# Memory rows transposed raw, their norm's gains in the weight tiles, and split memory kept in DRAM for a second layer

## The chip, the cores and the metric

The kernel runs on one core of one Trainium2 chip. The metric is the device time of one execution in microseconds (us), lower is better. A core has TensorE (PE, matmuls; PEld loads its weights), VectorE (DVE), ScalarE (ACT), GpSimd (POOL) and SyncE (SP, which here only issues DMA transfers). Each works through a row of instructions fixed when the program is built, and semaphores hold an instruction until what it reads is there.

## The reference, cut to what matters

Two encoder layers over x (512 tokens, D = 1024). In each, a token mixer and a cross attention of 4 heads to 256 memory tokens share one input projection and one output projection. The part that the change touches is the memory's way into K and V:

```python
def rmsnorm(x, g):
    y = x * lax.rsqrt(jnp.mean(x * x, axis=-1, keepdims=True) + EPS)
    return y * g
...
for i in range(DEPTH):
    h = rmsnorm(x, norm_g[i])
    mem_h = rmsnorm(mem, mem_norm_g[i])
    ...
    o_mem = memory_attention(q_mem, mem_h, w_mem_kv[i], mem_qn_g[i], mem_kn_g[i])
    y = jnp.concatenate([o_mix, o_mem], axis=-1) * jax.nn.silu(gate)
    x = x + jnp.einsum('bse,ed->bsd', y, w_out[i])
...
def memory_attention(q_mem, mem_h, w_kv, qn_g, kn_g):
    kv = jnp.einsum('bnd,de->bne', mem_h, w_kv).reshape(Bn, N, 2, MEM_HEADS, HEAD_DIM)
    k = rmsnorm(kv[:, :, 0], kn_g)
    v = kv[:, :, 1]
```

mem_norm_g has one row of 1024 gains for each layer; memory itself is the same in both layers. The norm of a memory row is a factor for each token (rm) and a gain for each of the 1024 features.

## The kernel before

All products are f32. Each operand is split in a high and a low part (fp32r), and a product is three matmuls: high times high and low times high of the activations (lines 176 and 177, mm_early), later high times the weights' low part (line 180, mm_late). The weights, 258 tiles of 128x1024 (`wl`), stream from DRAM over SP's queue (line 261). ACT casts a tile to its high part `wh` (line 323, Weights.hi), DVE subtracts to get the low part `wo` (line 333, Weights.lo); four such pairs are kept (RING). Some tiles are sums or differences of weight blocks, made by transfers from POOL that add in place (lines 261, 297 and 307).

A driver written in Python sets the order of every engine's row: matmul groups tick slots, and generators spawned with a delay (`drv.spawn`) put their next instructions in at a slot. A weight load is issued when the number of live tiles falls below a table's (KEEP).

The program begins with the memory. SP loads a row of gains and memory in pieces (lines 1056 to 1060), weights between them, then x's gains (line 654) and x's four tiles (line 1068). PE spreads the gains' row over the partitions by matmuls with ones (`spread`, line 1118). DVE multiplies memory by it (`times`, line 1128), PE transposes the product (`turn4`, line 536, into `xT`), and the result is split into `act` (`split`, lines 164 to 167; by `place_m`). ACT sums the squares of each memory row (`square`, line 1132) and POOL makes the tokens' factors of them (`factor`, lines 1137 to 1140: `rm` holds each factor plain, times QS and times 0.5). The factor of a token is applied behind the product, to K's sums of squares (line 629) and to V (line 707, `ev_v`). `mem_kv` runs eight groups of twelve 128x512 matmuls on `act`, each followed by its eviction. The transposes and splits of memory's four blocks are put between these groups by `ahead`; those of x (`prep`: squares in line 523, POOL's `rstd`, the product with `rstd` and gains in line 530, transposes) follow.

In the second layer `mem_norm(1)`, spawned during the first layer's output projection, loads memory and its gains again, normalizes it in full on DVE (line 530 into `m`), transposes it (16 transposes, in PE's row among the output projection's matmuls) and splits it; `mem_kv(1, ...)` then uses no factor.

Of the kernel before, what the change touches and what calls it, by code (L numbers as in the profile page):

```python
# [10 lines left out]
F32 = mybir.dt.float32  # L11
# [19 lines left out]
PD = 2  # L31
EO = 2, 2, 1, 2, 2, 1
# [99 lines left out]
def trunk_kernel(ctx: ExitStack, tc: tile.TileContext, x, mem, wall, norm_g, mem_norm_g, gcol,  # L132
# [63 lines left out]
    class Weights:  # L196
# [66 lines left out]
        def dma(self, most=9):  # L263
            while self.allocs and self.live < KEEP_C.get(self.allocs[0][0][0], KEEP[self.allocs[0][2]]) and most:
# [7 lines left out]
                self.load(nc.sync, self.tile[key], d)  # L272
# [40 lines left out]

        def hi(self, force=False):
# [8 lines left out]
            A.copy(wh, self.tile[self.items[i]])  # L323
            self.hi_at.append(self.g)
            self.op.append((wh, wo))
            return True

        def lo(self):
            i = self.n_lo
            self.n_lo += 1  # L330
            wh, wo = self.op[i]
            key = self.items[i]
            V.tensor_tensor(wo, self.tile[key], wh.bitcast(F32), ALU.subtract)  # L333
            self.lo_at[key] = self.g
            self.use(key)
# [153 lines left out]
    gc = pool.tile([128, 10], F32, name="gc")  # L489
    gk = pool.tile([128, 3], F32, name="gk")  # L490
# [5 lines left out]
    ones = tabs[0:1, 0:128]  # L496
    V.memset(half, -0.5)
    V.memset(ones, 1.0)
    A.activation(small.tile([128, 1], F32, tag="sm1", name="warm"), half[:, 0:1], AF.Exp)

    class Act:


        def __init__(self, n):
            per = 1024 // n
            self.tiles = [[m4(F32R, "act").rearrange("p (k t) -> p k t", k=per) for _ in range(8 // per)] for _ in range(2)]
# [152 lines left out]
    def mem_norm(layer):  # L659
        row_load("m", mem_norm_g[layer:layer + 1, :])  # L660
        t = [m4(name="m") for _ in range(2)]
        for b in range(2):
            nc.sync.dma_start(t[b], mem[b * 128:(b + 1) * 128])
        t = [halves(v) for v in t]
        yield MEM_D
        norm_2(t[0], rm[:, 0:1], rows["m"])
        yield 1
        norm_2(t[1], rm[:, 1:2], rows["m"])
        M = Act(NM)
        for b in range(2):  # L670
            for j in range(2):
                norm_3(t[b], M, b * 128, j)
            yield 1
        Ms[layer] = M

# [8 lines left out]
    def mem_kv(layer, M, mid=None):  # L684
# [4 lines left out]
        def ev_k(b, p):  # L689
            r = head_sq(p) if layer else head_sq(p, by=rm[:, 2 + b:3 + b])  # L690

            def rest():
                if not layer:
                    G.tensor_scalar(r, r, rm[:, b:b + 1], None, ALU.mult)
# [9 lines left out]
        def ev_v(b, p):  # L704

            t = s2(name="vr") if layer else raw[:, b * 512:b * 512 + 512]
            A.activation(t, p, AF.Copy, scale=0.5 if layer else rm[:, 4 + b:5 + b])
# [346 lines left out]
    nc.scalar.dma_start(ident, ident_d)  # L1054
    row0 = m4(name="row0")[0:1, :]
    nc.sync.dma_start(row0, mem_norm_g[0:1, :])
    nc.sync.dma_start(mt[0][:, 0:512], mem[0:128, 0:512])
    W.dma(2)
    nc.sync.dma_start(mt[1], mem[128:256])
    nc.sync.dma_start(mt[0][:, 512:1024], mem[0:128, 512:1024])  # L1060
    W.dma(2)
    row_load("x", norm_g[0:1, :])
    W.dma(2)
# [3 lines left out]
    for c in range(4):  # L1067
        nc.sync.dma_start(xt[c], xv[c])
        if c % 2 and c < 3:
            W.dma(2)  # L1070
# [41 lines left out]
    row = [at("row") for _ in range(2)]  # L1112

    def spread(j, *cols):

        for c in cols:
            cs = slice(256 * c, 256 * c + 256)
            T.matmul(row[j][:, cs], ones, row0[:, 512 * j + 256 * c:512 * j + 256 * c + 256], start=True, stop=True, skip_group_check=True)

    spread(0, 0, 1)  # L1120
    mb, M = [halves(t) for t in mt], Act(NM)
    ss = [sm(2, "ss") for _ in range(2)]
    mg = {}

    def times(b, j):

        t = mg[b, j] = s2(name="mg")
        V.tensor_tensor(t, mb[b][j], row[j], ALU.mult)
# [13 lines left out]
    def place_m(b, j, act=True, p=None):  # L1142

        cs = slice(b * 128, (b + 1) * 128)
        split(M.block(0, j, cs), M.block(1, j, cs), p or turn4(mg[b, j], None, None), act)
# [12 lines left out]
    for b, j in ((1, 0), (0, 1), (1, 1)):  # L1158
        square(b, j)
    for b in range(2):  # L1160
        times(b, 1)
        factor(b)

    def ahead(u, b):
# [5 lines left out]
        if (u, b) == (0, 1):  # L1170
            place_m(0, 1)
            place_m(1, 1)

    drv.spawn(prep(), PD)
# [293 lines left out]
    drv.spawn(mem_norm(1), MEM_B)  # L1468
# [318 lines left out]
```

## Time and profile before

| what | value |
|---|---|
| time before, median of 3 runs | 941.91 us (941.63 to 941.92) |
| profiled execution: time / span | 942.24 us / 940.5 us |
| PE busy | 932.8 us, 99% |
| DVE / ACT / POOL busy | 798.6 / 691.3 / 346.0 us |
| PE busy in the first 23.5 us | 21.01 us |
| DMA | 207.15 MB, mean 220 GB/s; 354 GB/s in the first 23.5 us |

In the rows below, a timeline row begins with the start in us and the time the row spans, then engine, line, operation, what is written and read, shapes and count; in brackets stands the idle time before it and what ended it. A row of several instructions (x4) is one block. A matmul's duration runs past the start of the next one, so the distance of two starts is what a matmul costs. A row of the windows has, for each engine, the busy time and the count, then the granted clock, the DMA share (1.0 and more is full) and GB/s.

### The profile page before, as it was taken

What the parts mean: (1) busy time and instruction counts of PE and PEld (TensorE: products, weight loads), DVE (VectorE), ACT (ScalarE), POOL (GpSimd) and SP (SyncE); (2) the same over time, 40 slices, a digit from 0 to 9 for tenths busy, and PEclk for the clock granted to TensorE, in tenths of its full rate; (3) what the DMA queues carried; (4) which work ended last, traced back from release to release, by engine and by line L of the source; (5) the groups of instructions that cost most, each with busy time, mean ns of one, the idle gap of its engine ahead of it and who ended that gap; (6) DMA issues with size and microseconds to landing.
All of it is one profiled execution on the core that took longest, in us unless ns stands there. A gap on an engine that the chain in (4) does not pass through costs nothing.

```text
span 940.5 us, 16300 instructions
## 1 busy us (share of the span) xinstructions
PE 932.8 (99%) x5500; PEld 819.9 (87%) x5500; DVE 798.6 (85%) x1442; ACT 691.3 (74%) x1720; POOL 346.0 (37%) x494
## 2 busy tenths in 40 slices
PE   8999999999999999999999999999999999999998
PEld 6889888888888888888889998888988999999886
DVE  6898676879888888889788899977998998689977
ACT  7775788677768686867675667637878887789774
POOL 3411425455554545463836111114262440111123
PEclk9999999999999999999999999999999999999999
DMA  9999937869787878696867889979985686785777
GB/s 355 386 259 336 299 91 190 278 139 256 158 250 147 260 154 268 158 268 136 249 165 206 246 200 243 305 229 326 270 203 122 166 239 168 199 221 126 190 173 179
DMA packets 89429, 207.15 MB, mean 220 GB/s; under 512 B 25217, under 2 KB 34689, under 8 KB 89346
## 3 DMA queue, kind: packets, MB, share of 16 engines
q1 hardware_dynamic: 68818, 140.64, 43.4%
q0 software_dynamic: 19520, 63.97, 36.9%
q10 hardware_dynamic: 1008, 1.51, 0.4%
q8 instruction: 43, 0.70, 0.3%
q14 instruction: 40, 0.33, 0.1%
HBM read 158.31 MB, written 11.08 MB: 180 GB/s over the span
## 4 chain that ended last, share of the span: by engine, by line
PE 91%; DVE 4%; DMA 3%; ACT 1%; issue 0%; SPq 0%; DVEq 0%; ACTq 0%
PE pj L176 24%; PE pj L177 24%; PE pj L180 23%; PE qT L641 2%; DMA og<-od 2%; PE ptb L1616 1%; PE sa L1302 1%; PE oo L1410 1%; PE pt L1389 1%; DMA wl<-in_wall_dram 1%; PE xT L536 1%; PE sa L1298 1%; DVE wo L333 1%; PE ob L180 1%; PE ob L177 1%; PE ob L176 1%
## 5 line engine op out<-in xcount | busy, mean ns | idle before, releaser
L333 DVE TENSOR_TENSOR wo<-wl,wh 128x1024 fp32r<-128x1024 f32 x258 | 316.4, 1232 | 7.0 <-ACT wh L323 6.8
L323 ACT CAST wh<-wl 128x1024 fp32r<-128x1024 f32 x258 | 271.7, 1060 | 29.7 <-PE pj L177 15.6
L176 PE MATMUL pj<-wh,hS 128*128 128x512 f32 (+1 forms) x416 | 154.3, 380 | 0.0
L177 PE MATMUL pj<-wh,hS 128*128 128x512 f32 (+1 forms) x416 | 148.9, 367 | 0.0
L176 PE MATMUL pj<-wh,h 128*128 128x512 f32 (+1 forms) x312 | 115.2, 378 | 0.0
L177 PE MATMUL pj<-wh,h 128*128 128x512 f32 (+1 forms) x312 | 111.7, 367 | 0.0
L484 POOL TENSOR_TENSOR rstd<-mse,half 128x4 f32<-128x4 f32 (+2 forms) x98 | 103.0, 1051 | 8.2
L180 PE MATMUL pj<-wo,hS 128*128 128x512 f32 (+1 forms) x416 | 99.5, 366 | 0.0
L177 PEld LDWEIGHTS pj<-wh,hS 128*128 128x128 f32 x416 | 78.7, 189 | 11.3
L176 PEld LDWEIGHTS pj<-wh,hS 128*128 128x128 f32 x416 | 78.6, 189 | 11.1 <-DVE sn L420 0.2
L483 POOL TENSOR_SCALAR mse<-hss 128x4 f32<-128x4 f32 (+1 forms) x88 | 46.1, 524 | 103.2 <-ACT junk L629 95.5
L180 PEld LDWEIGHTS pj<-wo,hS 128*128 128x128 f32 x416 | 72.4, 189 | 13.1
L629 ACT ACTIVATE junk<-sn 128x128 f32<-128x128 f32 x264 | 79.3, 311 | 2.2 <-DVE sn L411 2.1
L1246 POOL TENSOR_TENSOR ta<-sn,tabs 128x128 f32<-128x128 f32 (+1 forms) x64 | 35.9, 567 | 120.1 <-DVE sn L634 92.8
L398 ACT COPY sn<-pj 128x512 f32<-128x512 f32 x122 | 67.2, 590 | 16.6 <-PE pj L180 15.8
L180 PE MATMUL pj<-wo,h 128*128 128x512 f32 (+1 forms) x312 | 74.5, 365 | 0.0
L307 POOL DMA_DIRECT2D wl<-wl x34 | 30.2, 898 | 114.8 <-DVE wo L333 74.6
L261 POOL DMA_DIRECT2D wl<-in_wall_dram x40 | 38.1, 968 | 81.6 <-DMA wl<-in_wall_dram 35.3
L420 DVE TENSOR_TENSOR sn<-pj,sn 128x512 f32<-128x512 f32 x89 | 60.8, 684 | 7.1 <-PE pj L180 6.6
L177 PEld LDWEIGHTS pj<-wh,h 128*128 128x128 f32 x312 | 59.0, 189 | 8.4
L176 PEld LDWEIGHTS pj<-wh,h 128*128 128x128 f32 x312 | 59.0, 189 | 8.2
L180 PEld LDWEIGHTS pj<-wo,h 128*128 128x128 f32 x312 | 54.3, 189 | 9.7
(283 smaller groups left out, 2366.7 us busy)
## 6 DMA issues: line engine op xcount, KB each, us to landing
wl<-in_wall_dram SPq DMA_DIRECT2D x224, 512.0 KB, 7.5
wl<-wl POOLq DMA_DIRECT2D x68, 512.0 KB, 5.5
wl<-in_wall_dram POOLq DMA_DIRECT2D x44, 512.0 KB, 8.3
od<-o SPq DMA_DIRECT2D x11, 256.0 KB, 5.1
og<-od SPq DMA_DIRECT2D x10, 256.0 KB, 9.8
x<-in_x_dram SPq DMA_DIRECT2D x4, 512.0 KB, 9.0
v0d<-sn SPq DMA_DIRECT2D x8, 256.0 KB, 10.5
acc<-in_x_dram POOLq DMA_DIRECT2D x8, 256.0 KB, 7.1
```

The source lines that it names most:

```text
L176: T.matmul(o, a, b, start=start, stop=False, skip_group_check=True)
L177: T.matmul(o, c, d, start=False, stop=False, skip_group_check=True)
L180: T.matmul(o, a, b, start=False, stop=stop, skip_group_check=True)
L261: queue.dma_start(t, wall[d], **how)
L323: A.copy(wh, self.tile[self.items[i]])
L333: V.tensor_tensor(wo, self.tile[key], wh.bitcast(F32), ALU.subtract)
L398: A.copy(t, b)
L420: V.tensor_tensor(t, b, t, ALU.subtract if q == "12" else ALU.add)
L483: G.tensor_scalar(e, ss, EPS, None, ALU.add)
L484: G.tensor_tensor(r, e, half[:, 0:n], ALU.pow)
L629: A.activation(jk, p[:, j * 128:(j + 1) * 128], AF.Square, scale=by, accum_out=ss[:, j:j + 1])
L1246: G.tensor_tensor(ta[:, 0:n], xn[:, 0:n, 0:32], ropeA[:, 0, b, s0:s0 + n], ALU.mult)
```

## The change

- Memory is transposed raw. The row of gains, its eight spreading matmuls and the four products on DVE go away. The gains of both layers are loaded as 16 rows of 128 (`gm`), transposed once by PE (`gt`) and copied into `gmc`: one column for each 128 features.
- The gains go into the memory's weight tiles: a tile of 128x1024 holds two blocks of features, so ACT makes `wh` in two halves with a scale column each, and DVE makes `wo` in two halves as weights times gain minus `wh`. There are 16 such tiles, 8 in each layer.
- The token's factor is now applied in both layers behind the product; POOL multiplies K's factor by `rm` in the second layer too (two small operations).
- The split memory of the first layer (four `act` tiles, 512 KB each) is written to DRAM (`md`) by `keep_m`, and `mem_again` reads it back for the second layer. Its two memory loads, row of gains, norm, 16 transposes and splits go away.
- The first transfers are smaller: half a weight tile, a quarter of memory, the second half, and then weight tiles and quarters of memory in turn; x's gains come behind six weight tiles.
- The identity is made by POOL (affine_select) on cleared columns instead of being loaded. PE runs six matmuls on the cleared columns first (WARM).
- The first block of memory is cast and subtracted in two halves; the squares of memory go behind the third and fourth block's transposes. At most 10 weight tiles are live up to the third slot (START_KEEP).

The diff, cut to its core:

```diff
+WARM, START_KEEP, KEEP_M = 6, 10, 5
 ...
-            A.copy(wh, self.tile[self.items[i]])
+            key = self.items[i]
+            if key[1] == "P" and PLAN[key[0]] != "O1":
+                for c, g in self.gains(key):
+                    A.activation(wh[:, c], self.tile[key][:, c], AF.Copy, scale=g)
+            else:
+                A.copy(wh, self.tile[key])
 ...
+                for c, g in self.gains(key):
+                    V.scalar_tensor_tensor(wo[:, c], self.tile[key][:, c], g, wh[:, c].bitcast(F32), ALU.mult, ALU.subtract)
 ...
-    def mem_norm(layer):
 ...
+    def mem_again():
+        M = Ms[1] = Act(NM)
+        for n, t in enumerate(M.flat):
+            nc.sync.dma_start(t.bitcast(F32), md[n])
+        yield 1
 ...
-    nc.scalar.dma_start(ident, ident_d)
+    nc.scalar.dma_start(gm, mem_norm_g.rearrange("l (k p) -> (l k) p", p=128))
+    G.affine_select(ident, zero, [[-1, 128]], ALU.not_equal, 1.0, base=0, channel_multiplier=1)
 ...
+    for _ in range(WARM):
+        T.matmul(idle[:, 0:128], zero, zero, start=True, stop=True, skip_group_check=True)
+    T.transpose(gt, gm, ident[0:16, 0:16])
+    V.tensor_copy(gmc, gt)
 ...
-    square(0, 0)
-    times(0, 0)
-    spread(1, 0)
-    p = turn4(mg[0, 0], None, None)
-    spread(1, 1)
     W.hi(True)
-    place_m(0, 0, False, p)
     W.hi(True)
+    place_m(0, 0, (slice(0, 2), slice(2, 4)), False)
     W.lo()
-    times(1, 0)
     W.lo()
-    for b, j in ((1, 0), (0, 1), (1, 1)):
-        square(b, j)
-    for b in range(2):
-        times(b, 1)
-        factor(b)
 ...
         if (u, b) == (0, 1):
             place_m(0, 1)
+            square(0, 0)
+            square(0, 1)
+            factor(0)
+        if (u, b) == (1, 0):
             place_m(1, 1)
+            square(1, 0)
+            square(1, 1)
+            factor(1)
+    def keep_m():
+        for n, t in enumerate(M.flat):
+            nc.sync.dma_start(md[n], t.bitcast(F32))
+            yield 2
+    drv.spawn(keep_m(), KEEP_M)
 ...
-    drv.spawn(mem_norm(1), MEM_B)
+    drv.spawn(mem_again(), MEM_B)
```

Three places of the rows, before and after. First ACT from its first transfer to the squares of the first keys (`junk`); `sq` are squares of memory (`m`) and of `x`, `act` are the casts of memory's blocks. Before:

```order
L1054 DMA ident<-in_ident_dram 128x128
L1132 ACTIVATE sq,ss<-m 128x512
L323 CAST wh<-wl 128x1024 x2
L1132 ACTIVATE sq,ss<-m 128x512 x3
L164 CAST act<-xT 128x4x128
L323 CAST wh<-wl 128x1024 x2
L164 CAST act<-xT 128x4x128 x2
L323 CAST wh<-wl 128x1024 x2
L523 ACTIVATE sq,ss<-x 128x512 x4
L629 ACTIVATE junk,hss<-pj,rm 128x128 x4
```

After:

```order
L1067 DMA gm<-in_mem_norm_g_dram 16x128
L337 ACTIVATE wh<-wl,gmc 128x512 x4
L165 CAST act<-xT 128x4x128
L337 ACTIVATE wh<-wl,gmc 128x512 x4
L165 CAST act<-xT 128x4x128
L1141 ACTIVATE sq,ss<-m 128x512 x2
L337 ACTIVATE wh<-wl,gmc 128x512 x4
L546 ACTIVATE sq,ss<-x 128x512 x2
L165 CAST act<-xT 128x4x128
L1141 ACTIVATE sq,ss<-m 128x512 x2
L546 ACTIVATE sq,ss<-x 128x512 x2
L652 ACTIVATE junk,hss<-pj,rm 128x128 x4
```

The squares of memory and the casts of the weights have changed places with the casts of memory's blocks: the last of these now stands behind the squares of x's first tile.

Then DVE in the same stretch, where the last row is the product of x's first tile. Before:

```order
L1128 TENSOR_TENSOR mg<-m,row 128x512
L166 CAST act<-xT 128x4x128
L167 TENSOR_TENSOR act<-xT,act 128x4x128
L333 TENSOR_TENSOR wo<-wl,wh 128x1024
L1128 TENSOR_TENSOR mg<-m,row 128x512
L333 TENSOR_TENSOR wo<-wl,wh 128x1024
L1128 TENSOR_TENSOR mg<-m,row 128x512 x2
L167 TENSOR_TENSOR act<-xT,act 128x4x128
L333 TENSOR_TENSOR wo<-wl,wh 128x1024 x2
L167 TENSOR_TENSOR act<-xT,act 128x4x128 x2
L333 TENSOR_TENSOR wo<-wl,wh 128x1024 x2
L530 SCALAR_TENSOR_TENSOR x<-x,rstd,row 128x512 x2
```

After:

```order
L1135 COPY gmc<-gt 128x16
L167 CAST act<-xT 128x2x128
L168 TENSOR_TENSOR act<-xT,act 128x2x128
L167 CAST act<-xT 128x2x128
L168 TENSOR_TENSOR act<-xT,act 128x2x128
L351 SCALAR_TENSOR_TENSOR wo<-wl,gmc,wh 128x512 x4
L168 TENSOR_TENSOR act<-xT,act 128x4x128
L351 SCALAR_TENSOR_TENSOR wo<-wl,gmc,wh 128x512 x4
L168 TENSOR_TENSOR act<-xT,act 128x4x128 x2
L351 SCALAR_TENSOR_TENSOR wo<-wl,gmc,wh 128x512 x4
L553 SCALAR_TENSOR_TENSOR x<-x,rstd,row 128x512 x2
```

The products of memory and gains are gone, and each pair of weight tiles is four halves. As before, the last two subtractions of memory's blocks stand together, ahead of the third pair of tiles, and these ahead of x's product; the second subtraction reads what ACT's last cast of memory writes.

Last SP, from the loads of x's four tiles to the first store of v0 (`v0d`, which waits for data of the first values of x). Before:

```order
L1068 DMA x<-in_x_dram 128x1024 x2
L261 DMA wl<-in_wall_dram 128x1024 x2
L1068 DMA x<-in_x_dram 128x1024 x2
L261 DMA wl<-in_wall_dram 128x1024 x18
L1183 DMA v0d<-sn 128x512 x2
L261 DMA wl<-in_wall_dram 128x1024
```

After:

```order
L1087 DMA x<-in_x_dram 128x1024 x2
L262 DMA wl<-in_wall_dram 128x1024 x2
L1087 DMA x<-in_x_dram 128x1024 x2
L262 DMA wl<-in_wall_dram 128x1024 x14
L1186 DMA md<-act 128x1024 x2
L262 DMA wl<-in_wall_dram 128x1024 x2
L1186 DMA md<-act 128x1024
L262 DMA wl<-in_wall_dram 128x1024
L1186 DMA md<-act 128x1024
L262 DMA wl<-in_wall_dram 128x1024
L1199 DMA v0d<-sn 128x512 x2
L262 DMA wl<-in_wall_dram 128x1024
```

The four writes of `act` to `md` stand among the last weight loads ahead of that store. On PE, at the boundary of the layers, the two rows of eight transposes of `m` (line 536), each behind a group of twelve matmuls of the output projection, are gone; nothing else in that stretch of PE's row changes.

More of the change, by code (lines that the diff above doesn't have):

```diff
@@ L312, in sum, with gains @@
             return False
+        def gains(self, key):
+            n = 8 * (PLAN[key[0]] == "T2b") + 2 * key[2]
+            return [(slice(512 * h, 512 * h + 512), gmc[:, n + h:n + h + 1]) for h in range(2)]
         def hi(self, force=False):
@@ L489, in trunk_kernel @@
     gc = pool.tile([128, 10], F32, name="gc")
+    gmc = pool.tile([128, 16], F32, name="gmc")
     gk = pool.tile([128, 3], F32, name="gk")
@@ L505, in __init__ @@
             per = 1024 // n
-            self.tiles = [[m4(F32R, "act").rearrange("p (k t) -> p k t", k=per) for _ in range(8 // per)] for _ in range(2)]
+            self.flat = [m4(F32R, "act") for _ in range(16 // per)]
+            ts = [t.rearrange("p (k t) -> p k t", k=per) for t in self.flat]
+            self.tiles = [ts[:8 // per], ts[8 // per:]]
             self.part = [[t[:, k] for t in ts for k in range(per)] for ts in self.tiles]
@@ L1110, in setup @@
             yield 1
[L1112 to L1120, printed above, removed]
+    idle, gt = at("idle"), at("gt")[:, 0:16]
+    for _ in range(WARM):
+        T.matmul(idle[:, 0:128], zero, zero, start=True, stop=True, skip_group_check=True)
+    T.transpose(gt, gm, ident[0:16, 0:16])
+    V.tensor_copy(gmc, gt)
     mb, M = [halves(t) for t in mt], Act(NM)
     ss = [sm(2, "ss") for _ in range(2)]
[L1123 to L1128, printed above, removed]
     def square(b, j):
```

68 lines of the change are left out of this document (33 added, 35 removed).

## The prediction

> **What bounds the kernel.** I read the page's first two parts, then the waits of TensorE (PE) over the whole span, then the timeline of the engines where PE is not busy, which is the start.
>
> ```profile
> span 940.5 us, 16300 instructions
> ...
> PE 932.8 (99%) x5500; PEld 819.9 (87%) x5500; DVE 798.6 (85%) x1442; ACT 691.3 (74%) x1720; POOL 346.0 (37%) x494
> ```
>
> ```profile
> PE row L1118 <- DMA row<-in_mem_norm_g_dram: 2.3, 1, 2.3
> PE pmt L768 <- DVE pmT L774: 0.7, 1, 0.7
> ```
>
> PE is busy in 99% of 940.5 us. It waits 2.3 us for the first row and at no other place more than 0.7 us, so a change counts only where it takes matmuls out of PE's row, or moves PE's first 24 us. The row of each engine is fixed when the program is built; an engine that waits holds all that stands behind it.
>
> The start on PE:
>
> ```profile
> 2.26 2.89 PE L1118 MATMUL row<-row,tabs 1*128 1x256 f32 x6 [2.26 <-DMA row<-in_mem_norm_g_dram]
> 5.08 1.11 PE L536 MATMUL xT<-ident,mg 128*128 128x128 f32 x4
> ...
> 7.28 0.80 PE L176 MATMUL pj<-wh,act 128*128 128x512 f32 x1
> 7.87 0.63 PE L177 MATMUL pj<-wh,act 128*128 128x512 f32 x1
> ...
> 10.43 0.63 PE L177 MATMUL pj<-wh,act 128*128 128x512 f32 x1
> 10.86 1.05 PE L536 MATMUL xT<-ident,mg 128*128 128x128 f32 x4
> 11.56 1.42 PE L180 MATMUL pj<-wo,act 128*128 128x512 f32 x4
> 12.82 0.39 PE L176 MATMUL pj<-wh,act 128*128 128x512 f32 x1
> ...
> 15.03 1.03 PE L536 MATMUL xT<-ident,mg 128*128 128x128 f32 x8
> ...
> 16.83 0.39 PE L176 MATMUL pj<-wh,act 128*128 128x512 f32 x1
> ...
> 19.70 0.39 PE L176 MATMUL pj<-wh,act 128*128 128x512 f32 x1
> ...
> 21.52 1.07 PE L180 MATMUL pj<-wo,act 128*128 128x512 f32 x4
> 22.71 1.06 PE L536 MATMUL xT<-ident,x 128*128 128x128 f32 x8
> 23.53 0.48 PE L176 MATMUL pj<-wh,act 128*128 128x512 f32 x1
> ```
>
> The eight row matmuls (2.26 and, the last two, 6.13) and the transposes fill PE until the first real matmul at 7.28. The groups of twelve matmuls (hi times both parts of the memory, then four with the weights' low part) that make the memory's K and V start at 7.28, 12.82, 16.83, 19.70, then 23.53: call them G0 to G4. From 7.28 to 10.43 a matmul of 128x512 comes every 0.43 us ((10.43 - 7.87)/6), and in G3 every 0.23 ((21.52 - 19.70)/8); the four from 11.56 take 0.32 each. So PE's clock came up near 12 us, 4.7 us after G0's start. Between G3's end and G4 stand the transposes of x's first tile, at 22.71; they wait for VectorE. From 23.5 on there is hardly a gap, so what G4 gains or loses the end gains or loses.
>
> The same stretch on ScalarE (ACT) and VectorE (DVE):
>
> ```profile
> 3.81 0.63 ACT L1132 ACTIVATE sq<-m 128x512 f32<-128x512 f32 x1 [1.59 <-DMA m<-in_mem_dram]
> ...
> 6.17 1.04 ACT L323 CAST wh<-wl 128x1024 fp32r<-128x1024 f32 x1 [1.64 <-DMA wl<-in_wall_dram]
> 7.47 1.04 ACT L323 CAST wh<-wl 128x1024 fp32r<-128x1024 f32 x1 [0.25 <-DMA wl<-in_wall_dram]
> ...
> 11.95 0.59 ACT L164 CAST act<-xT 128x512 fp32r<-128x512 f32 x1 [1.19 <-PE xT L536]
> 12.43 2.00 ACT L323 CAST wh<-wl 128x1024 fp32r<-128x1024 f32 x2
> 15.72 1.07 ACT L164 CAST act<-xT 128x512 fp32r<-128x512 f32 x2 [1.29 <-issue]
> ...
> 18.58 0.64 ACT L523 ACTIVATE sq<-x 128x512 f32<-128x512 f32 x1
> ...
> 19.20 0.63 ACT L523 ACTIVATE sq<-x 128x512 f32<-128x512 f32 x1
> ```
>
> ```profile
> 6.24 0.69 DVE L166 CAST act<-xT 128x512 fp32r<-128x512 f32 x1 [1.21 <-PE xT L536]
> 6.96 0.69 DVE L167 TENSOR_TENSOR act<-xT,act 128x512 fp32r<-128x512 f32 x1
> 7.57 1.21 DVE L333 TENSOR_TENSOR wo<-wl,wh 128x1024 fp32r<-128x1024 f32 x1
> ...
> 21.18 1.43 DVE L530 SCALAR_TENSOR_TENSOR x<-x,rstd,row 128x512 f32<-128x512 f32 x2 [1.05 <-POOL rstd L484]
> ```
>
> ACT is free between 7.47 and 11.95 but for squares; DVE's last wait before G4 is for x's statistics (21.18).
>
> **The change, part by part.**
>
> *First transfers and row matmuls, a gain at G0.* The first matmul now needs half a weight tile, a quarter of the memory and no row. The first quarter of memory was there at 3.81 and the first weight tile, 512 KB further in the queue, at 6.17, so 256 KB cost 1.2 us here; with half a weight tile going first and 0.4 us earlier, memory lands at about 4.6 and the weight's second half at 5.8. Transposes at 4.6 need no product with the row (mg, 0.69 us). From 5.08 to 6.24 the transposes took 1.16; the high part is now made in two halves (0.35 each), and G0 starts at 4.6 + 1.16 + 0.4 = 6.2, say 6.3: 1.0 us earlier. G0 needs the tables of gains on the partitions (gmc), which take the place of the identity's transfer and come before 4 us; the identity itself is made by POOL.
>
> *G1.* G0 to G1 took 5.54 (12.82 - 7.28), most of it at the slow clock. If the clock counts from the first real matmul, G1 starts at 6.3 + 5.5 = 11.8, less about 0.2 us for the second row matmuls that no longer press: 11.6, a gain of 1.2. If the six idle matmuls at about 1 us bring the clock up earlier, G1 is at 10.8; if the clock comes up no earlier than it did, at 12.4.
>
> *ACT's row between G1 and G4, a loss.* Weight tiles of the memory are now scaled in halves. A half with a scale taken from a tile has no row at the start; the nearest of its size, squares, follow each other in 0.62 us (18.58, 19.20), so four halves are about 2.4 us where two whole casts took 2.0 (12.43). More than that, the row's order changes. After the cast of the third block of memory come two squares of memory, four halves for the next two weight tiles, two squares of x, and only then the cast of the fourth block, on which G3 depends; before, both casts stood together at 15.72. So, from G1 = 11.6: the third block's transposes stand behind G1's eight matmuls, 2.2 us later (12.82 to 15.03), its cast 0.7 us behind these (15.03 to 15.72), at 14.5; cast 0.6, squares 1.2, four halves 2.4, squares 1.2: the fourth block's cast starts at 19.9. Even if PE were faster, it stands behind x's first tile: 7.5 tiles of 512 KB follow the second weight tile, which lands near 7.4, at 1.30 us each (6.17 to 7.47): 17.2, and two squares end at 18.4. G3 starts about 0.7 us behind the cast: 20.6 (19.1 at the least), against 19.70.
>
> *DVE's row behind it.* The subtraction of that block (0.6, as from 6.96 to 7.57) is followed by four halves of wo. One half is a product with a scalar and a subtraction, as x's in row 21.18: two in 1.43, 0.69 apart; four take 2.8, where two whole ones took 2.4. Only then comes x's product. The cast at 19.9 frees it at 20.5; 20.5 + 0.6 + 2.8 = 23.9 is x's start instead of 21.18. Row 21.18 to row 23.53 is 2.35, so G4 starts at 26.2: 2.7 us later than before. The fastest case (the cast at 18.4, set by x's landing) gives 19.0 + 0.6 + 2.8 + 2.35 = 24.75, +1.2; the slowest (G1 at 12.4) 27.0, +3.5. I take +2.6, a little under the middle value, since an early clock weighs more than a late one.
>
> *Second layer's memory, a gain.* At the boundary stand 2 x 8 transposes of m, in PE's row without a gap:
>
> ```profile
> 615.28 1.07 PE L180 MATMUL pj<-wh,y 128*128 128x512 f32 x4
> 616.19 1.03 PE L536 MATMUL xT<-ident,m 128*128 128x128 f32 x8
> 616.98 0.48 PE L176 MATMUL pj<-wh,y 128*128 128x512 f32 x1
> 617.29 0.40 PE L177 MATMUL pj<-wo,y 128*128 128x512 f32 x1
> ```
>
> Four matmuls from 615.28 end their pitch at 616.19; the next matmul comes at 616.98 and the one behind it 0.31 later where the pitch is 0.23. So eight transposes are 0.79 + 0.08 = 0.87 us, sixteen 1.74. The products, casts and subtractions that leave DVE and ACT there gain nothing, PE not waiting for them; the weight tiles' halves there cost 0.2 us of ACT and of DVE per tile, hidden behind the casts and subtractions that leave. The second layer reads four tiles (2 MB) instead of 1.5 MB, far ahead of use.
>
> *Memory kept in DRAM, a small loss.* The first layer writes 2 MB more, from SP's queue, ahead of the last four weight loads before the first store of v0:
>
> ```profile
> 15.80 22.46 SPq L261 DMA_DIRECT2D wl<-in_wall_dram  x18
> 53.70 0.92 SPq L1183 DMA_DIRECT2D v0d<-sn  x2
> ```
>
> ```profile
> 23.50:47.00 23.50, 23.50 (x119) 19.72 (x118) 21.03 (x27) 17.82 (x37) 9.85 (x15) 1.00 1.03 387
> 47.00:70.00 23.00, 23.00 (x107) 19.04 (x106) 22.42 (x33) 17.85 (x26) 3.52 (x4) 1.00 1.05 258
> ```
>
> At 387 GB/s, 2 MB are 5.4 us of a DMA system that is full from 23.5 to 70. SP's own row has room: it issued its last weight load before 38.3 and then stood until 53.7. PE never waited for a tile in this stretch, and all of PE is now 2 to 3 us later, which gives the loads that much. Lower end 0; upper end 5.4 - 2.6 = 2.8, if tiles were there only just in time. I take 0.2, near the lower end, because PE has no wait at all in the row of its waits.
>
> *POOL.* It clears 128 columns and makes the identity before anything else. The nearest rows for a first operation:
>
> ```profile
> 10.23 0.41 POOL L1137 TENSOR_TENSOR mse<-ss 128x1 f32<-128x1 f32 x1 [9.79 <-ACT sq L1132]
> ...
> 12.51 0.20 POOL L1137 TENSOR_TENSOR mse<-ss 128x1 f32<-128x1 f32 x1
> ```
>
> The first took 0.41, the same one later 0.20; so the identity costs 0.2 us or, if it is several times dearer than the first one, 2; starting near 0.9 it ends by 2.9, before memory lands at 4.6: nothing. But POOL stood idle up to 10.23, and a slow start of its own before that would not be seen in these rows; the third rival takes that. [...]
>
> *Sum.* +2.6 - 1.74 + 0.2 = +1.06 us. The profiled execution took 942.24 in all, 0.33 above the median of 941.91; 942.24 + 1.06 = 943.3 against it, 943.0 against the median.
>
> [...]
>
> **Rivals.**
>
> *Faster: the gain of the start stays.* If memory's fourth block does not wait for ACT as I read it, because halves and squares are quicker or x lands early, G4 keeps G1's gain of 1.2. For it: PE's row itself is shorter, by eight row matmuls. Against it: x's squares, which stand ahead of it, end at 18.4 by the count of tiles. It decides at the start of the fourth block's cast: by 17.2 nothing is lost (17.2 + 0.6 + 0.6 + 2.8 + 2.35 is the old 23.5), by 16.0 the whole 1.2 stays, so x would have to land 1 to 2 us earlier than in my count. Time: 941.91 - 1.2 - 1.74 = 939.0.
>
> *Slower: the writes of memory delay weight tiles.* For it: a full DMA system (1.03 and 1.05 above), 5.4 us more in it. Against it: PE's waits of zero there. If the tiles had 3 us to spare, of 5.4 less 2.6 nothing is left; with none, 2.8. At 2.2 us: 943.0 + 2.0 = 945.0. It would show as PE gaps between 40 and 70 us.
>
> *Slower: POOL's identity comes late.* All transposes wait for it. It costs nothing up to 4.6 us, and POOL is known to work only from 10.23 on; halfway, at 7.4, transposes start 2.8 us later, G1 goes from 11.6 to about 14, and G4 comes about 2.5 later than forecast: 945.5. Against it: no row of POOL shows a long first operation. It decides from 4.6 us on.
>
> *The boundary does not pay.* If PE then waits for the tiles or for the weights' halves there, the 1.74 is lost: 944.7. Against it, ACT idles there and the reads are issued far ahead.
>
> **How the numbers follow.** Forecast (G4 +1.2 to +3.5, with the boundary's gain and 0.2 for the writes: -0.3 to +2.0 in all, 941.6 to 943.9): 0.47. Gain stays, with what else of the landings I count wrongly: 0.20. Writes: 0.13. Late identity: 0.12. Boundary: 0.08. A change of 0.2%, 1.9 us, is about what a measurement of this kernel can tell from none: the forecast lies inside it, but for its upper end, to which I give 0.03. So faster 0.20, same 0.44, slower 0.36. The range leaves out the lower half of the first rival and the upper part of the slower ones: 939.2 to 945.6. The likeliest case's own range is 941.6 to 943.9.
>
> **What would show it.** Right: G0 at 6.3, a PE gap of 1 to 3 us before x's first transposes, x's product on DVE at 23 to 25, G4 at 25 to 27; no transposes at the boundary and no gap in their place. Wrong: a first transpose later than 5 us (identity), a fourth block's cast before 18 us (the gain stays), PE waits of over 0.5 us between 40 and 70 us (writes), or a PE wait for act behind 600 us.

## The result, and the profile after

The changed kernel takes 950.71 us (median of 5, 950.58 to 953.72), the kernel before 941.91 on the same chip (median of 5, 941.0 to 942.73). The ratio is 1.0105, with an interval of 1.0089 to 1.012: 8.8 us slower. The profiled execution took 950.71 us.

The first lines of the page after:

```profile
span 948.9 us, 16302 instructions
...
PE 932.1 (98%) x5489; PEld 818.8 (86%) x5489; DVE 794.2 (84%) x1448; ACT 694.3 (73%) x1732; POOL 354.3 (37%) x498
```

PE is busy 0.7 us less than before, in a span that is 8.4 us longer. The loss is waits of PE, so I followed the start of the same matmul in both traces. "Offset" below is the start of a matmul in one kernel's profiled execution minus its start in that of before; where it grows, PE has waited, and where it falls, work has left PE's row. G4, at 23.53, is the first group behind the start.

| offset, us, at before's time | 12.8 (G1) | 23.5 (G4) | 60 | 104 | 235 | 614 | 625 | 650 | 680 |
|---|---|---|---|---|---|---|---|---|---|
| after | +0.15 | +4.29 | +4.93 | +8.35 | +8.28 | +7.30 | +5.51 | +6.47 | +8.34 |

So of 8.3 us the start makes 4.3, a stretch from 60 to 104 makes 3.4, the boundary gives back 1.8, and the second layer's memory then takes 2.8. The rest nearly cancels: 0.6 between G4 and 60 (PE waits for x's later tiles), and 1.0 given back in small steps up to 614, which were not followed further.

The start on PE, from the timeline after:

```profile
5.52 0.47 PE L177 MATMUL pj<-wh,act 128*128 128x512 f32 x1 [0.61 <-DVE act L167]
...
6.94 0.51 PE L177 MATMUL pj<-wh,act 128*128 128x512 f32 x1 [0.54 <-ACT wh L337]
...
8.54 0.80 PE L177 MATMUL pj<-wh,act 128*128 128x512 f32 x1 [0.86 <-ACT wh L337]
...
12.97 0.63 PE L177 MATMUL pj<-wh,act 128*128 128x512 f32 x1
...
22.25 0.50 PE L177 MATMUL pj<-wh,act 128*128 128x512 f32 x1 [1.39 <-ACT act L165]
...
27.00 1.07 PE L559 MATMUL xT<-ident,x 128*128 128x128 f32 x8 [1.21 <-issue]
27.82 0.48 PE L177 MATMUL pj<-wh,act 128*128 128x512 f32 x1
```

G0 starts 1.76 us earlier than before (5.52 against 7.28), but then waits twice for its weights: 0.54 for the second half of the first tile and 0.86 for the second tile. G1 (12.97) is already 0.15 late. G3 (22.25) waits 1.39 us for ACT's cast of memory's fourth block, and the transposes of x's first tile (27.00) wait for DVE.

ACT and DVE, after:

```profile
6.16 0.72 ACT L337 ACTIVATE wh<-wl,gmc 128x512 fp32r<-128x512 f32 x1 [1.06 <-DMA wl<-in_wall_dram]
7.76 1.34 ACT L337 ACTIVATE wh<-wl,gmc 128x512 fp32r<-128x512 f32 x2 [0.88 <-DMA wl<-in_wall_dram]
11.51 0.59 ACT L165 CAST act<-xT 128x512 fp32r<-128x512 f32 x1 [2.40 <-PE xT L559]
11.99 2.56 ACT L337 ACTIVATE wh<-wl,gmc 128x512 fp32r<-128x512 f32 x4
16.23 0.58 ACT L165 CAST act<-xT 128x512 fp32r<-128x512 f32 x1 [1.68 <-PE xT L559]
...
17.95 2.55 ACT L337 ACTIVATE wh<-wl,gmc 128x512 fp32r<-128x512 f32 x4
20.40 0.62 ACT L546 ACTIVATE sq<-x 128x512 f32<-128x512 f32 x1
...
21.63 0.57 ACT L165 CAST act<-xT 128x512 fp32r<-128x512 f32 x1
```

```profile
22.23 0.69 DVE L168 TENSOR_TENSOR act<-xT,act 128x512 fp32r<-128x512 f32 x1 [4.69 <-ACT act L165]
22.84 2.73 DVE L351 SCALAR_TENSOR_TENSOR wo<-wl,gmc,wh 128x512 fp32r<-128x512 f32 x4
25.49 1.40 DVE L553 SCALAR_TENSOR_TENSOR x<-x,rstd,row 128x512 f32<-128x512 f32 x2
```

The fourth block's cast stands at 21.63, behind two squares of memory, four halves of `wh` in 2.55 us and two squares of x; DVE then subtracts (22.23), makes four halves of `wo` in 2.73 and comes to x's product at 25.49 instead of 21.18.

The granted clock in three stretches (third figure from the right; before it the busy times of PE, PEld, DVE, ACT and POOL, behind it the DMA share and GB/s):

```profile
4.40:7.81 3.41, 2.13 (x8) 0.94 (x7) 2.79 (x6) 1.46 (x3) 0.00 (x0) 1.00 0.88 279
7.82:14.60 6.78, 6.06 (x16) 4.88 (x17) 4.01 (x7) 4.33 (x7) 0.00 (x0) 0.50 1.03 410
14.70:18.00 3.30, 3.07 (x16) 2.23 (x15) 1.48 (x3) 1.77 (x6) 0.00 (x0) 1.00 1.04 403
```

Behind the six idle matmuls the clock came up at 4.40 us, but it fell again at 7.81, after G0's waits, for twice 3.41 us, over all of what was left of G0 and half of G1. In the trace of before it came up at 12.09 and stayed.

The stretch from 60 to 110, after: PE's two waits, then what stood on DVE and POOL ahead of them.

```profile
91.27 0.39 PE L177 MATMUL pj<-wh,hS 128*128 128x256 f32 x1 [1.29 <-DVE sn L440]
...
110.54 0.66 PE L1228 MATMUL qT<-ident,sn 128*128 128x128 f32 x4 [1.59 <-DVE sn L657]
```

```profile
86.52 1.23 DVE L298 TENSOR_TENSOR wl<-wl 128x1024 f32<-128x1024 f32 x1 [1.49 <-DMA wl<-in_wall_dram]
87.67 0.68 DVE L440 TENSOR_TENSOR sn<-pj,sn 128x512 f32<-128x512 f32 x1
...
109.79 0.69 DVE L657 TENSOR_TENSOR sn<-sn,rstd 128x512 f32<-128x512 f32 x1 [5.77 <-POOL rstd L504]
```

```profile
106.18 0.93 POOL L262 DMA_DIRECT2D wl<-in_wall_dram  x1 [8.61 <-DMA wl<-in_wall_dram]
...
108.71 1.05 POOL L504 TENSOR_TENSOR rstd<-mse,half 128x4 f32<-128x4 f32 x1
```

PE's 91.27 waits for the sum `sn` on DVE, behind DVE's sum of two weight tiles (L298, 86.52), which waits for a load from DRAM. PE's 110.54 waits for `sn` (109.79), that for `rstd` on POOL (108.71), and POOL stood 8.61 us at a transfer that adds to a tile whose load had not landed.

The second layer: before's rows on ACT and DVE, then those after.

```profile
645.14 2.01 ACT L323 CAST wh<-wl 128x1024 fp32r<-128x1024 f32 x2
...
649.10 0.69 DVE L634 TENSOR_TENSOR xn<-pj,rstd 128x512 f32<-128x512 f32 x1 [1.26 <-POOL rstd L484]
```

```profile
652.38 2.56 ACT L337 ACTIVATE wh<-wl,gmc 128x512 fp32r<-128x512 f32 x4
...
653.37 1.06 PE L559 MATMUL xT<-ident,acc 128*128 128x128 f32 x8 [0.72 <-DVE acc L553]
...
656.77 0.69 DVE L657 TENSOR_TENSOR xn<-pj,rstd 128x512 f32<-128x512 f32 x1 [1.67 <-POOL rstd L706]
...
674.42 0.39 PE L177 MATMUL pj<-wh,hS 128*128 128x256 f32 x1 [1.82 <-DVE sn L440]
```

The two tiles' halves take 2.56 us of ACT instead of 2.01. `xn` on DVE waits 1.67 us for its factor instead of 1.26 and comes 7.67 us later than before, though PE was only 5.51 behind at 625; from `xn` on DVE has hardly a gap (busy 17.28 of the 17.70 us from 656.70 to 674.40) up to the `sn` for which PE waits 1.82 (674.42).

### The profile page after: what moved, and what is told of

The parts are those of the page before. It is cut to its first block, busy times and chain, and to the rows that moved or that the text cites. A ratio compares the mean times of both kernels' runs of the same rounds, so it can differ in the third digit from the quotient of the medians.

```text
span 948.9 us, 16302 instructions
## 1 busy us (share of the span) xinstructions
PE 932.1 (98%) x5489; PEld 818.8 (86%) x5489; DVE 794.2 (84%) x1448; ACT 694.3 (73%) x1732; POOL 354.3 (37%) x498
## 4 chain that ended last, share of the span: by engine, by line
PE 86%; DVE 5%; DMA 3%; ACT 3%; issue 1%; POOL 1%; SPq 0%; DVEq 0%; ACTq 0%; POOLq 0%
PE pj L177 22%; PE pj L178 22%; PE pj L181 22%; PE qT L664 3%; DMA wl<-in_wall_dram 2%; PE sa L1318 2%; PE oo L1426 2%; PE pt L1405 1%; PE ptb L1632 1%; PE sa L1314 1%; DVE wo L353 1%; DMA wl<-wl 1%; PE ob L181 1%; PE ob L178 1%; PE ob L177 1%
## 5 line engine op out<-in xcount | busy, mean ns | idle before, releaser
L353 DVE TENSOR_TENSOR wo<-wl,wh 128x1024 fp32r<-128x1024 f32 x242 | 295.9, 1226 | 6.6 <-ACT wh L339 6.6
L339 ACT CAST wh<-wl 128x1024 fp32r<-128x1024 f32 x242 | 255.9, 1061 | 23.9 <-PE pj L178 15.0
```

What stands on the lines that cost most here:

```text
L339: A.copy(wh, self.tile[key])
```

## The experiments

Times are medians; "G4", "614" and so on are offsets as above, from one profiled execution of each kernel. Behind the start the clock fell to half (0.50 in the windows of e6 below) in some of these executions, for 3.41 us each time: at 23.72, 91.98 and 675.66 in e1, at 80.39 and 674.31 in e2, at 22.99 in e3, at 22.70 in e4 and at 672.76 in e6. Where PE had no other wait such a fall cost 1.3 to 1.5 us, and the offsets behind it contain it.

**e1: no idle matmuls.**

```diff
-WARM, START_KEEP, KEEP_M = 6, 10, 5
+WARM, START_KEEP, KEEP_M = 0, 10, 5
```

> The changed kernel without the six idle matmuls. Theory (they bring the clock up at 4.4, but PE waits for the second weight tile until 8.5 and loses it again from 7.8 to 14.6, so they bring nothing by G1): the clock comes up once, near 12 to 13, G1 starts within 0.6 us of 12.97 and the time is within 1 us of 950.7. Rival (without them the clock comes up later still): G1 later than 13.6 and over 951.5.

952.03 us, 1.0103 [1.0085, 1.0121]. The clock comes up at 13.48; G1 stands at +0.60 (after +0.15), but x's product on DVE is at 25.20 (after 25.49) and G4 at +4.19 (after +4.29). In these two executions the idle matmuls bring a few tenths by G1 and nothing by G4. From G3 on e1's falls of the clock are part of its offsets, so that behind G4 the two do not compare.

**e2: the fourth block placed with the third**, so that both casts stand together on ACT as before.

```diff
         if (u, b) == (0, 1):
             place_m(0, 1)
+            place_m(1, 1)
             square(0, 0)
 ...
         if (u, b) == (1, 0):
-            place_m(1, 1)
             square(1, 0)
```

> The fourth block of memory is transposed and cast right behind the third, as in the kernel before, so ACT's cast no longer stands behind the squares of x's first tile. Theory (ACT's order sets G3 and G4): the third and fourth cast stand together at 16.2 and 16.7, G3 starts near 20.2 instead of 22.25, x's product on DVE near 23.4 instead of 25.49, and G4 near 25.7 instead of 27.82; the whole is 2.1 us shorter, 948.6. Rival (the late G1 and the late clock alone set G4): G4 stays within 0.5 us of 27.8, 950.7.

949.57 us, 1.0075 [1.0058, 1.0092]. G4 falls from +4.29 to +0.85. Part of this is the clock, which came up for good at 12.12, with G1 at -0.53; e8 below, with the same order and G1 at +0.34, has G4 at +2.12. So the order of ACT's row carries some 2 us of the start's loss. Little of it reaches the end: the median is 1.1 us under that of after, and the profiled execution, 950.9, was the longest of the four. PE reaches the next weight tiles earlier and waits for them there:

```profile
80.61 2.07 PE L181 MATMUL pj<-wo,h 128*128 128x512 f32 x4 [2.35 <-DVE wo L353]
```

At the end of this wait the clock fell for 3.41 us (80.39 to 83.80), and at 85 the offset is +6.80, where after has +6.38. At 614 e2 is still 1.3 us ahead of after (+6.03 against +7.30); its second fall, at 674.31, takes that. So in this execution the clock, and not the weights' lateness alone, takes what the order gave.

**e3: nothing written to DRAM.** The second layer loads memory again and transposes it raw; the gains stay in the weight tiles.

```diff
-    drv.spawn(keep_m(), KEEP_M)
 ...
-        for n, t in enumerate(M.flat):
-            nc.sync.dma_start(t.bitcast(F32), md[n])
+        for b in range(2):
+            for j in range(2):
+                norm_3(t[b], M, b * 128, j)
```

> Nothing is written to DRAM; the second layer loads memory again and transposes it raw (16 transposes, splits, no norm). Theory (the 2 MB of writes make weight loads late, and that stalls DVE's sum, POOL and PE between 84 and 110 us): the 3.3 us lost there on PE are gone, the boundary costs 1.7 again, and the 2.7 lost behind it come down to 1 to 2; in all 2.5 to 3 us shorter, near 948. Rival (the later start alone shifts loads and sums against each other): the waits between 84 and 110 stay, and with the transposes back the time is near 952.

949.61 us, 1.0078 [1.0063, 1.0093]. No growth is left between 60 and 614: the offset is +3.96 at 60 and +3.96 at 104, where after goes from +4.93 to +8.35. The boundary gives nothing (+2.95, +2.98), and the second layer costs 2.8 as after. The 3.4 us between 60 and 104 are the writes'.

**e4: the second layer's tiles without gains**, whole casts and subtractions as before.

```diff
-            if key[1] == "P" and PLAN[key[0]] != "O1":
+            if key[1] == "P" and PLAN[key[0]] not in ("O1", "T2b"):
```

> The gains of the second layer's memory are left out of its eight weight tiles, which are cast and subtracted whole as before (so the second layer's memory has no gains). Theory (the halves cost 0.56 us of ACT and 0.38 of DVE per pair of tiles on a chain that PE has come to wait for): of the 2.7 us that PE loses between 646 and 675, some 2 are gone, 948.7. Rival (PE, 1.7 us earlier without the transposes, simply runs into the same chain earlier): the loss stays at 1.7 or more, 949.8 to 950.7.

948.23 us, 1.0067 [1.0052, 1.0082]. From 625 to 680 the offset grows by 0.8 (+4.31 to +5.11) instead of 2.8. So the halves cost 2.0 us there. The 0.8 that are left fit the token factor, which now scales ACT's squares of K (four `junk` rows in 1.37 us instead of 1.0) and adds operations to POOL; that was not tried apart.

**e5 and e7: the kernel before, with the four writes alone**, of 512 KB and of 64 KB each.

```diff
+    def keep_m():
+        for n, t in enumerate(M.tiles[0] + M.tiles[1]):
+            nc.sync.dma_start(md[n].rearrange("p (k t) -> p k t", k=M.per), t.bitcast(F32))
+            yield 2
+    drv.spawn(keep_m(), 5)
     drv.spawn(prep(), PD)
```

In e7 the transfer is `nc.sync.dma_start(md[n][:, 0:128], t.bitcast(F32)[:, 0, 0:128])`.

> The kernel before, which also writes its four tiles of split memory to DRAM at the same place of SP's row and never reads them. Theory (writes alone make tiles late): PE waits of about 3 us between 80 and 105 appear, 945. Rival (only together with the later start): under 0.5 us, 942 to 942.4.

> The kernel before with the same four writes as in the run of the kernel before with writes, but of 64 KB each, an eighth of the bytes. Theory (bytes in a full DMA system): of the 4.6 us there, at most 0.6 are left, 942.5. Rival (a write holds up SP's row or its queue, whatever its size): 3 us or more are left, 945 or more.

e5: 946.76 us, 1.0049 [1.0034, 1.0064]. e7: 942.84 us, 1.0007 [0.9997, 1.0016]. Nothing else differs from before; in e5 G4 does not move (+0.03). In e5 the offset is +0.03 at 60 and +5.21 at 104; in e7, whose clock came up 1.2 us earlier by chance (G1 -0.57), it goes from -0.42 to +1.72. SP's row in e5:

```profile
34.35 1.61 SPq L1179 DMA_DIRECT2D md<-act  x2
36.96 10.35 SPq L261 DMA_DIRECT2D wl<-in_wall_dram  x2
...
56.04 0.45 SPq L1096 DMA_DIRECT2D tabs<-in_mask_dram  x1
...
67.49 0.56 SPq L1099 DMA_DIRECT2D grA<-in_kn_a_dram  x1
```

Two weight loads took SP from 36.96 to 47.31, and the small tables behind the first store of v0, which before issued between 55.18 and 57.21, come 3.8 us apart, the last at 67.49. DVE and PE in e5, then in e7:

```profile
74.91 0.21 DVE L1105 TENSOR_SCALAR grA<-grA 128x96 f32<-128x96 f32 x1 [2.51 <-DMA grA<-in_qn_a_dram]
...
77.51 1.19 PE L180 MATMUL pj<-wo,h 128*128 128x512 f32 x4 [1.97 <-DVE wo L333]
...
88.56 0.39 PE L176 MATMUL pj<-wh,hS 128*128 128x256 f32 x1 [1.23 <-DVE sn L420]
```

```profile
59.54 0.33 SPq L261 DMA_DIRECT2D wl<-in_wall_dram  x1
...
74.10 0.21 DVE L1105 TENSOR_SCALAR grA<-grA 128x96 f32<-128x96 f32 x1 [4.55 <-DMA grA<-in_qn_a_dram]
...
76.70 1.20 PE L180 MATMUL pj<-wo,h 128*128 128x512 f32 x4 [1.60 <-DVE wo L333]
```

DVE waits for a small table (`grA`, 2.51 us, and 4.55 in e7), and behind it in DVE's row stands the `wo` for which PE waits (1.97, and 1.60). What held the tables stands in SP's own waits between 30 and 70 us (us in total, how often, the longest), in e5 and then in e7:

```profile
SPq L261 <- DMA md<-act: 9.6, 1, 9.6
...
SPq L1097 <- DMA md<-act: 3.4, 1, 3.4
```

```profile
SPq L261 <- DMA md<-act: 13.1, 2, 8.8
```

SP waits in two ways. A weight load (L261) that goes into a buffer that held `act` stands until the write from this buffer has landed: 9.6 us in e5, 8.8 and 4.3 in e7 (the second is the load at 59.54), and 7.2 in the changed kernel. The first write landed 12.6 us after its issue in e5 (34.35 to 46.93) and 11.7 us after it in e7 (34.10 to 45.81), so this wait hardly depends on the write's own bytes. Further, SP's transfers take eight semaphores in turn (101 and 104 to 110 in the trace of after), so that each waits for the one eight places ahead of it; with four writes in the row, two of the tables stand eight places behind a write: L1097, which waits 3.4 us here, and L1099 (in after the third write and the second table are on 109, the fourth write and the last table on 101). So a write delayed what SP issued behind it here, and the first to suffer was not a weight tile.

How much hangs on the row and how much on the bytes is less clear. With an eighth of the bytes 2.1 of the 5.2 us stay in the one execution traced. The medians say less: e5 is 4.9 us above the kernel before, e7 0.9, with an interval that includes no change, and 942.84 is near what the theory of the bytes expected (942.5) and far from its rival's 945.

**e6: the writes later**, at slot 60.

```diff
-WARM, START_KEEP, KEEP_M = 6, 10, 5
+WARM, START_KEEP, KEEP_M = 6, 10, 60
```

> The changed kernel with the four writes of memory put 55 slots later in SP's row, behind the loads of the stretch in which DMA is full. Theory (the same bytes cost nothing where DMA has room): the waits of 0.4 to 1.8 us between 37 and 110 go, 3 to 4 us shorter, near 947. Rival (memory's four tiles hold buffers 100 us longer, and loads then wait for buffers): waits of the same size appear between 60 and 140, 950 or more.

949.45 us, 1.0078 [1.0057, 1.01], with single executions from 946.68 to 951.22. The waits between 60 and 104 are gone (+3.48, +3.48); two smaller losses come later, +0.5 at 143 and +1.1 at 229. The writes now stand between 203 and 226, so the second comes just behind them; the first comes ahead of any write and fits the rival, tiles held longer, which was not shown. Here the clock came up at 10.57 and stayed up to the second layer: G1 stands at 11.78, x's product at 24.02 and G4 at +2.81. In the second layer the clock fell:

```profile
671.33 0.39 PE L177 MATMUL pj<-wh,hS 128*128 128x256 f32 x1 [1.79 <-DVE sn L440]
```

```profile
669.00:672.70 3.70, 1.91 (x16) 1.68 (x15) 3.70 (x5) 3.70 (x7) 0.00 (x0) 1.00 1.09 230
672.77:676.16 3.39, 3.39 (x19) 3.39 (x18) 3.39 (x5) 2.56 (x10) 0.72 (x1) 0.50 0.94 310
```

After one wait of 1.79 us PE ran at half clock from 672.76 for 3.41 us, and the offset went from +5.25 at its start to +6.76 at its end, 1.5 us.

**e8: e2 and e6 together.**

> Both mendings together: the fourth block cast behind the third, and the late writes. If they add up: the start costs 1 to 2.1 us, the writes nothing, the boundary gives 1.75 back, the second layer's halves take 2.7: 944 to 945.5. If PE, being earlier, runs into tiles that are not there: waits at 75 to 85 us as with the mended order alone, 947.

947.76 us, 1.0069 [1.0053, 1.0086]. G4 +2.12, 60 +3.43, 104 +3.44, 235 +5.42 (the losses of e6 at 143 and 229 again), 625 +2.69, 680 +5.52. Against after, with nearly the same G1, the order gains 2.2 us at G4 and keeps 1.5 at 60 (+3.43 against +4.93): the rest is lost on x's next tiles, whose squares still stand behind squares of memory on ACT. That is what e11 takes away.

**e9 and e10: e8 without gains in any tile, and without gains in the second layer's alone.** e9 has `if False:` in place of the condition, e10 the condition of e4.

> Order and writes mended as in the run before, and the gains left out of all sixteen weight tiles of memory, which are cast and subtracted whole (memory has no gains in either layer). Theory (the halves are what is left of the start's loss and most of the second layer's): G4 and x's third tile 1 to 1.5 us earlier than with both mendings (offsets against the kernel before of 0.5 to 1.5 at 24 and 35 us instead of 2.1 and 3.2), the second layer 2 us better: 944 to 945. Rival (the loads' order and the late second weight tile make the start's loss): the start stays at 2 to 3, 945.5 to 946.5.

> Order and writes mended, and the gains left out of the second layer's eight tiles alone. If the parts add up: 947.8 less the 2.0 that the halves of the second layer cost by themselves, 945.8 (945 to 946.5). The difference to the run without any gains is then what the first layer's halves cost.

e9: 945.44 us, 1.0029 [1.0018, 1.0041]; e10: 945.35 us, 1.0031 [1.002, 1.0042]. From 625 to 680 both grow by 0.8 us, e8 by 2.8: 2.0 us again for the second layer's halves. In the first layer they cost 0.3 (at 60, e9 +2.86, e10 +3.13), although e9 loses the early G0 (+0.08 instead of -1.37). So the theory for the start fails: without any halves G4 is still at +1.70 in e9, where it expected 0.5 to 1.5.

**e11: e8, and the squares of memory in ACT's idle time**, three behind the first casts of weights, one behind the next.

```diff
+    square(0, 0)
+    square(1, 0)
+    square(0, 1)
+    factor(0)
 ...
             place_m(1, 0)
             W.hi(True)
             W.hi(True)
+            square(1, 1)
+            factor(1)
 ...
             place_m(1, 1)
-            square(0, 0)
-            square(0, 1)
-            factor(0)
-        if (u, b) == (1, 0):
-            square(1, 0)
-            square(1, 1)
-            factor(1)
```

> Both mendings, and the squares of memory moved back into ACT's idle time ahead of the second block's cast (three behind the first weight halves, one behind the next four). Theory (what is left of the start's loss is ACT's row: two squares of memory, 1.2 us, ahead of x's): x's product 1.2 us earlier, G4's offset against the kernel before 0.5 to 1 instead of 2.1; 946.5. Rival (loads set it): offset still near 2, 947.8.

946.37 us, 1.0048 [1.0031, 1.0065], from 943.5 to 949.8; the profiled execution took 944.88. PE and ACT:

```profile
15.08 1.07 ACT L165 CAST act<-xT 128x512 fp32r<-128x512 f32 x2
...
18.51 0.62 ACT L546 ACTIVATE sq<-x 128x512 f32<-128x512 f32 x1
...
22.64 1.06 PE L559 MATMUL xT<-ident,x 128*128 128x128 f32 x8 [0.68 <-issue]
```

Casts at 15.08, x's squares at 18.51, x's transposes on PE at 22.64 against 22.71 before: G4 -0.08. With the order mended and memory's squares out of the way nothing is left of the start's loss, at 60 either (-0.05); 0.8 us of that is an earlier clock (G1 -0.48, e8 +0.34). Later come +2.3 by 235, -1.0 in small steps up to 614, -1.8 at the boundary and +2.9 in the second layer: +2.44 at 680.

**e12: e11 with the writes at slot 40.**

```diff
-WARM, START_KEEP, KEEP_M = 6, 10, 60
+WARM, START_KEEP, KEEP_M = 6, 10, 40
```

> As the run before, with the writes 20 slots earlier, when the weight loads of the full stretch are issued but before the small transfers of the first layer's attention. Theory (late writes cost 1.5 us near 229 us because they stand among small transfers that are waited for): that wait goes and no other comes, 945. Rival (any place costs about as much): 946 to 947.5. With the second layer's halves still costing more than the transposes gave, it would not be under 942 in either case.

944.23 us, 1.0017 [1.0008, 1.0026], the best form of the change, and still not faster than before. The writes, now between 128 and 157, make no PE wait around them (104 +1.76, 235 +1.70); the 0.7 that comes between 60 and 104 stands ahead of them. G4 is +1.01, with the clock at half speed from 7.35 to 14.18. With G1 where e8 has it (+0.44, +0.34), the squares' place is worth 2.4 us at 60 (+1.06 against +3.43). 614 +0.74, 625 -1.05, 680 +1.81: the boundary's 1.8 us are less than the 2.9 that the second layer's gains and factors take behind it.

| kernel | median, us | 12.8 (G1) | 23.5 (G4) | 60 | 104 | 614 | 625 | 680 |
|---|---|---|---|---|---|---|---|---|
| e3, no writes | 949.61 | -0.06 | +3.47 | +3.96 | +3.96 | +2.95 | +2.98 | +5.81 |
| e5, writes alone | 946.76 | +0.08 | +0.03 | +0.03 | +5.21 | +4.50 | +4.50 | +4.51 |
| e6, writes later | 949.45 | -1.04 | +2.81 | +3.48 | +3.48 | +4.19 | +2.40 | +6.70 |
| e10, order, later, second layer plain | 945.35 | +0.28 | +1.85 | +3.13 | +3.13 | +4.25 | +2.46 | +3.26 |
| e12, order, squares, writes at 40 | 944.23 | +0.44 | +1.01 | +1.06 | +1.76 | +0.74 | -1.05 | +1.81 |

## Why the prediction was wrong, step by step

The sum was +2.6 - 1.74 + 0.2 = +1.06; the trace has +4.3 for the start, -1.8 for the boundary, +3.4 for the writes and +2.8 for the second layer's weights and factors, with +0.6 and -1.0 in between. Three terms of the sum were mis-sized: the writes (0.2 taken, 3.4 measured), the second layer's halves and factors (nothing taken, 2.8 measured) and the start (2.6 taken, 4.3 measured).

- *Memory kept in DRAM, a small loss*: the step that failed most. I took 0.2, with 2.8 as upper end, because PE showed no wait before and runs 2 to 3 us later now. The writes alone cost 5.2 us by 104 in e5, with no late start to hide them, and 3.4 in the changed kernel. A row of waits without PE says that nothing was late; it does not say how much later a transfer may come. I had also read that SP's row has room; but with the writes in it SP stands 9.6 us (e5; 7.2 in after) until a write has freed the buffer of the next weight load. And I looked for the delay at the wrong place, in weight tiles between 40 and 70 us. It came in the small tables and the loads issued behind the writes, and reached PE through DVE's and POOL's rows at 77 to 110.
- *Second layer's memory*: the boundary's gain was right (-1.79 for 1.74 forecast, and without a PE wait in its place). What I called hidden there was not: the weights' halves, "0.2 us of ACT and of DVE per tile", cost 2.0 us, by e4 against after and by e10 against e8. The work that leaves does not cover them, since ACT's squares of K, POOL's factor and `xn` stand behind the halves, and DVE is full from `xn` to `sn` (17.28 of 17.70 us). PE had nothing to spare there: in before this `sn` ended at 666.03 (665.35 and 0.68), and the matmul that waits 1.82 us for it after started at 666.08. That PE showed no wait hid it. The token factor in the second layer, to which I gave no price, fits the other 0.8.

```profile
665.35 0.68 DVE L420 TENSOR_TENSOR sn<-pj,sn 128x512 f32<-128x512 f32 x1
...
666.08 0.39 PE L176 MATMUL pj<-wh,hS 128*128 128x256 f32 x1
```

- *ACT's row between G1 and G4* and *DVE's row behind it*: the mechanism was right, and e2 and e11 show it: with both casts together G4 is at +0.85 (e2) or +2.12 (e8), and with memory's squares out of the way too at -0.08 (e11) or +1.01 (e12). The size holds where the clock was as assumed: e6 has G1 at 11.78, x's product at 24.02 and G4 at 26.34, for 11.6, 23.9 and 26.2 forecast. In after it is 4.3, outside my +1.2 to +3.5, because G1 came at 12.97: that is 1.37 later than the 11.6 of the sum, and 26.2 + 1.37 is 27.6, of the 27.82 measured.
- *First transfers* and *G1*: G0 came 0.8 earlier than forecast (5.52 for 6.3), but on the first half tile alone. The second tile was cast at 7.76, and in the wait for it (0.86 us, up to 8.54) the clock fell, at 7.81. I had the clock coming up early or late; I did not have it falling again. But the fall is not all: in e8 the clock came up once, at 12.41, and G1 stands at +0.34 as well, behind a wait of 1.41 us for the second tile. So the second tile's landing keeps G1 from gaining; the two parts were not separated.

*POOL* was right: the first rows of its timeline after have the identity at 1.00, in 0.29 us.

```profile
1.00 0.29 POOL L1068 TENSOR_SCALAR_AFFINE_SELECT ident<-tabs 128x128 f32<-128x128 f32 x1
```

So the rival of a late identity falls.

Of the other rivals, the one that the gain of the start stays falls in the changed kernel: the fourth block's cast is at 21.63, not before 17.2. In e11 it stands at 15.08 and nothing is lost. The rival of the writes was the right one, with a price too low; the boundary did pay.

## What to carry to other kernels

That PE waits for nothing in a stretch does not price a transfer put there (four writes cost 5.2 us by 104 in e5): see which loads are queued behind it on its row, which of them need its buffer, who reads them, and how long before use they land. When work moves from one place to another (a gain from the memory to its weights), price it at the new place, in the rows that end last there; here 16 transposes saved 1.8 us and 8 tiles in halves cost 2.0. Where a row's order decides, put the cast that PE waits for ahead of the squares that only a later factor needs (2.2 us at G4, e8 against after).

## What the runs showed of the hardware

- In these traces the clock fell after a short wait, for 3.41 us or twice that. One PE wait of 1.79 us (e6, 671.33) was followed by 3.41 us at half clock, which cost 1.5 us; G0's waits of 0.54 and 0.86 us in after were followed by two such stretches. Whole multiples of 3.41 us lie between the changes of the clock in after (4.40, 7.81 and 14.64: 1 and 2), e1 (13.48, 23.72, 91.98 and 675.66: 3, 20 and 171), e2 (12.12, 80.39 and 674.31: 20 and 174), e6 (10.57 and 672.76: 194) and e12 (7.35 and 14.18: 2).
- How the work fell into these steps differed from execution to execution. Of the ten executions with the six idle matmuls the clock came up early in four (after, e2, e11 and e12, at 3.94 to 5.29), and each time fell again; in the six others it came up at 10.57 to 13.52. Each of the eight falls behind the start came at the end of a step that held 1.39 (e1, up to 21.96) to 2.13 us (e2, 78.26 to 80.39) of one wait. That did not decide alone: behind 1.88 us within one step in e8 (22.95 to 24.83) and 1.76 in e12 (up to 667.88) the clock did not fall. That this makes the spread of single executions (946.68 to 951.22 in e6) fits, but was not shown.
- The smaller first transfers moved less in the same time in most executions: from 3.9 to 7.8 us 262 to 328 GB/s in the eleven that have them (after 262, e6 328), 328 to 371 in the three that do not (before 371, e7 328). No run changed the sizes alone.
- Four writes of 64 KB delayed PE by 2.1 us by 104 us (e7), four of 512 KB by 5.2 (e5), in one execution each; by the medians the kernels lost 0.9 and 4.9.
